# S5's two state scans issued at other places of the program, and HGRN2's scan steps taken in pairs

## The chip, the cores and the metric

The kernel runs on one core of one Trainium2 chip. The metric is device time in microseconds (us) of one execution, lower is better. A program of a core runs on five queues in parallel: PE (TensorE, matrix products), DVE (VectorE), ACT (ScalarE), POOL (GpSimd) and SP (SyncE, here only a queue that issues DMAs). POOL's queue carries DMA issues besides its arithmetic. Within a queue the instructions run in the order in which the program issued them; between queues they wait for one another by semaphores.

## What is computed

One inference step of a decoder of two layers, on 512 prompt positions and 64 sample positions (8 sequences of 8), 576 columns in all, width 1024, everything in float32. Layer 0 mixes tokens with HGRN2, layer 1 with S5. After the mixer, each layer has a SwiGLU and a per-layer embedding:

```python
def s5_mixer(x, h0_re, h0_im, ..., w_glu):
    bu = jnp.einsum('btgc,gpc->btgp', u, b_bar)            # 64 groups x 64 complex states
    bu = bu.at[:, 0].add(lam_bar * h0)
    _, h = lax.associative_scan(s5_combine, (a_el, bu), axis=1)   # h_t = lam_bar h_(t-1) + bu_t
    y = jnp.einsum('btgp,gcp->btgc', h, c_mat).real + d_skip * u
    y = jax.nn.gelu(y.reshape(bsz, t, D_MODEL))
    val, gate = jnp.split(y @ w_glu, 2, axis=-1)
    return val * jax.nn.sigmoid(gate), h_last.real, h_last.imag

# layer i, mixer = hgrn2 for i = 0, s5 for i = 1
x = layer_norm(ALPHA * x + mixer(x))
x = layer_norm(ALPHA * x + swiglu(x))
x = x + rms_norm((p_i @ w_proj) * sigmoid(x @ w_gate))
```

HGRN2 is a gated linear recurrence per head (8 heads of 128), computed chunkwise: products within a chunk, a state carried from chunk to chunk, and for the samples one step from the given states.

## The kernel before

**Matmuls and weights.** Every float32 weight product is made of three passes over a high and a low part (`mm3`, L295 to L299: L296 is high by high, L297 high weight by low activation, L298 low weight by high activation). A weight slot is 128x1024 numbers: a DMA loads it (`w_dma`, L217), ACT copies out the high part (`whi`, `w_conv`, L226), DVE subtracts to get the low part (`wlo`, `w_rest`, L250), and `w_rest` issues the DMA of a later slot at once. When these are issued is counted in products: `passed(n)`, called after each product, advances a counter, and conversions come due by it. The raw tile has two buffers, the converted slots a ring of `R_W` = 5 ("base") and, inside `more_weights`, some more ("ext", `WX` = 3 here). The first gated tiles of S5 use slots 118 to 125 of the weight order; slots 118 to 122 sit in the base ring, 123 to 125 in the ext ring, whose memory lies where the pools `op_pool` and `outer` lay.

**HGRN2 (from the start to about 340 us).** `hgrn()` projects head after head (`proj`), one yield for each `mm3`: 88 for an even head (it also makes V for two heads), 48 for an odd one. Meanwhile the scan of the head before is a generator (`scan`, L650), stepped after the yields whose numbers stand in `SCAN_AT` (first tuple for even h, second for odd). Its steps: 1 transposes four chunks of K2 (L658), copies them on ACT to `kT` and masks V on POOL; 2 transposes the samples' chunk (L665); 3 multiplies kT by V (L671) and carries the state; 4 and 5 make the sample states (L685); 6 to 9 make the attention of four chunks (L701, L706); 10 masks it on DVE (L710) and multiplies the sample queries (L716); 11 to 16 finish the head (L722 to L757). Head 7's scan runs later, after another list.

**S5 (about 890 to 1020 us).** The columns lie in two blocks of 288 (36 chunks of 8 positions). The stage runs in this order of the program, in `layer0_to_1`:

1. `z_part(0, o)` for eight octets of groups: products that give the chunks' inputs of block 0.
2. Block 0's scan, four quarters of 16 groups: `turn` (four DVE operations that rotate by a table), `run_on` (one DVE scan instruction and, where due, a copy of lengths), `turn` back.
3. Tiles `pj1` and `U`, loads of block 1's inputs, `ple_proj` (L964): 16 steps of two `mm3` and one ACT copy each, for the embedding of layer 1.
4. The DMA of the sample states `h0`, issued on POOL (L1620), then `z_part(1, o)`.
5. `last_samples`: h0 is scaled into the columns of block 0 (L1629), advanced on DVE, scaled on ACT and stored.
6. `lag_part(o)`, eight octets (L1471), copied out of PSUM by ACT; block 1's scan is the generator `last_states` (two yields for a quarter, nine steps in all), stepped after octets by `SL`.
7. `out_part(0, o)`, eight octets (L1444 with the states of block 0): DVE adds the product (`u<-u,mm`), ACT takes the GELU, SP writes it to DRAM and reads it back transposed, ACT and POOL split it into `xh` and `xl`. Block 1's scan is stepped after octets by `SO0`; what is left of it runs after the loop.
8. The gated tiles: for block and m, 48 passes (two units of 24) and `val * sigmoid(gate)`. Tiles (0,0) and (0,1) are multiplied at once in four PSUM banks (`GG` = 4). There are four banks in all for such products. At tile (0,3) `out_part(1, o)` comes first; it needs the states of block 1's scan.

The scan generator, whose steps are moved:

```python
        def last_states():
            for q in range(4):
                turn(1, q, True)
                run_on(1, q)
                yield
                turn(1, q, False)
                yield
            advance(po, chunk_state(63), ZL[:, :, 8])
            ...
            yield
```

Of the kernel before, what the change touches and what calls it, by code (L numbers as in the profile page):

```python
# [62 lines left out]
SY = ((6, 8), (8, 8), (6, 10), (6, 2))  # L63
QY = ((3, 3), (2, 5), (1, 3), (1, 2))
SPLIT_S5 = 14
SCAN_AT = ((2, 4, 10, 16, 20, 26, 30, 34, 38, 42, 46, 50, 54, 60, 68, 74), (2, 4, 6, 9, 12, 15, 17, 19, 21, 23, 26, 33, 34, 36, 41, 45))
QWAIT = 9
SIDE = 1
OCT = 1
TB = 3  # L70
SL = (0, 0, 1, 0, 1, 0, 1, 0)
SO0 = (0, 1, 0, 1, 0, 1, 0, 1)
YD = 4
WX = 3
AB = 2
GS = 3
SW = 64
GG = 4
LNEXP = "natural_log_exp_and_others"
# [60 lines left out]
def hybrid_decoder_kernel(ctx: ExitStack, tc: tile.TileContext, a: dict):  # L140
# [10 lines left out]
    def mm_bank():  # L151
        return bank("mm", 4)
# [110 lines left out]
    @contextmanager  # L263
    def more_weights(bufs, limit):

        with tc.tile_pool(name="wx", bufs=bufs) as pool:
            rings["ext"] = [pool, bufs, bufs, limit]
            yield
            assert pos["freed"] >= limit
            del rings["ext"]  # L270
# [3 lines left out]
    def take(n):  # L274
        p = pos["i"]
        pos["i"] += n
        return p
# [74 lines left out]
    def run(g):  # L352
        for _ in g:
            pass

    def step(g, n=1):
        for _ in range(n):
            if next(g, StopIteration) is StopIteration:
                return False
        return True  # L360

    def cols(blk):
        return slice(blk * NB, blk * NB + NB)
# [106 lines left out]
    def hgrn():  # L470
# [52 lines left out]
        def proj(h):  # L523
            if h % 2 == 0:
                p = take(16)
                V[h // 2] = hp.tile([128, 5, 256], FP32, tag="V", name="V", bufs=2)
                for i in range(5):
                    c = slice(i * 128, i * 128 + 128) if i < 4 else slice(T - 128, T)
                    ps = mm_bank()
                    for k in range(KD):  # L530
                        hi, lo = w_ap(p + 2 * k, 256)
                        mm3(ps[:, :256], xhih[:, k, c], xloh[:, k, c], hi, lo, k == 0, k == KD - 1)
                        yield
                    copy(V[h // 2][:, i, :], ps[:, :256])
                free_to(p + 16)
            d = hd[h] = {}

            yield from two_units(take(8))
            sides.append(decay(h, d, hd["ps"]))

            yield from two_units(take(8))
            sides.append(factors(d, hd["ps"]))
            yield from two_units(take(8))
            sides.append(queries(h, d, hd["ps"]))
# [217 lines left out]
        for h in range(H):  # L762
            at = SCAN_AT[h % 2]
            for n, _ in enumerate(proj(h)):
# [199 lines left out]
    def ple_proj(pj, pin):  # L964
        hi, lo = pin
        p = take(16)
        for m in range(KD):
            for blk in range(2):
                ps = mm_bank()
                run(unit(ps[:, :NB], p + 2 * m, [0, 1], lambda k, b: hi[:, k, cols(b)],  # L970
                         lambda k, b: lo[:, k, cols(b)], blk))
                copy(pj[:, m, cols(blk)], ps[:, :NB])
                yield
            free_to(p + 2 * m + 2)
# [540 lines left out]
    def turn(blk, q, back):  # L1515

        gs, n = slice(16 * q, 16 * q + 16), slice(1, 36 if blk else KA + 1)
        h, c, C, Z = (x[:, n] if len(x.shape) == 2 else x[:, :, n] for x in
                      (HS[blk][:, gs], s5["c"], s5["C"][:, gs], s5["Z"][:, gs]))
        tt(c[0:64], h[64:128], Z[64:128], OP.mult)  # L1520
        tt(c[64:128], h[0:64], Z[0:64], OP.mult)
        tt(h, h, C, OP.mult)
        tt(h, h, c, OP.add if back else OP.subtract)
# [5 lines left out]
    def run_on(blk, q):  # L1529
        h = HS[blk][:, 16 * q:16 * q + 16].rearrange("p g k -> p (g k)")  # L1530
        nc.vector.tensor_tensor_scan(h, s5["rho"][q % 2].rearrange("p g k -> p (g k)"), h, 0.0,
                                     op0=OP.mult, op1=OP.add)
        if (blk, q) < (1, 2):
            lengths((q + 2) % 4)
# [3 lines left out]
    def layer0_to_1():  # L1538
        right, wide, outer = ExitStack(), ExitStack(), ExitStack()
# [28 lines left out]
        op_pool = ExitStack()  # L1568
# [24 lines left out]
            elif o > 1:  # L1593
                step(tails[1], 2)
        settle(1)
        for q in range(4):
            turn(0, q, True)
            run_on(0, q)
            turn(0, q, False)
        left.close()  # L1600
        pj1 = left.enter_context(tc.tile_pool(name="pp1", bufs=1)).tile([128, KD, T], FP32, name="pj1")
        work = ExitStack()
# [10 lines left out]
        def samples(tag, n=1):  # L1613
            t = s5["zp"].tile([128, n, NG, 8], FP32, tag=tag, name="sm")
            return [t[:, i] for i in range(n)]

        proj = ple_proj(pj1, s5["pin"])
        run(proj)
        h0, = samples("phi")
        nc.gpsimd.dma_start(h0, a["h0"])  # L1620
# [34 lines left out]
        scan = last_states()  # L1655
# [10 lines left out]
        for o in range(8):  # L1666
            lag_part(o, mg[o])
            if o >= OCT:
                cl.append(octet(s5["zq"], cl_d, len(cl), "zw", 8))
            step(scan, SL[o])  # L1670
        for o in range(8):
            out_part(0, o, cl[o])
            y_start(0, o)
            step(scan, SO0[o])
            if o >= YD:
                step(y_loads[0, o - YD])
        y_start(0, 8)
        y_start(0, 9)
        for o in range(8 - YD, 8):
            step(y_loads[0, o])  # L1680
        run(scan)

        ln = None
        op_pool.close()
        outer.close()
        gp = work.enter_context(tc.tile_pool(name="gp", bufs=1))
        p0, pss = take(128), []
        with more_weights(WX, (p0 + 128) // 8):
            for blk, m in [(b, m) for h in (0, 4) for b in range(2) for m in range(h, h + 4)]:
                p = p0 + 16 * m  # L1690
                if (blk, m) == (0, 3):
                    st.update(queue=nc.sync, load=LOAD_MM, split=SPLIT_MM)
                    for n in range(8):
                        out_part(1, n, cl[n])
                        y_start(1, n)
                    y_start(1, 8)
                    y_start(1, 9)
                    wide.close()
                    ln = open_norm(3, 4, False)
                    for n in range(m):  # L1700
                        ln[0].added(n)
                while len(pss) < 2:
                    new = [mm_bank() for _ in range(1 if blk or m else GG)]
                    go(units([ps[:, :NB] for ps in new], p + 8 * len(pss), list(range(KD)), x_hi, x_lo, blk))
                    pss += new
                psv, psg = pss[:2]
                pss = pss[2:]
                if blk == 1:
                    free_to(p + 16)
                if (blk, m) == (0, 3):  # L1710
                    for n in range(KD):
                        step(y_loads[1, n])
                s = gp.tile([128, NB], FP32, tag="gs", name="gs", bufs=GS)
                tables()
                act(s, psg[:, :NB], ACT.Sigmoid)
                tt(s, s, psv[:, :NB], OP.mult)
                residual(m, blk, s)
                if ln:
                    ln[blk].added(m)
# [176 lines left out]
```

## Time and profile before

| | us |
|---|---|
| median of 3 runs | 1583.01 (1582.04 to 1585.63) |
| the profiled execution, its own time | 1582.62 |
| its span, first to last instruction | 1580.8 |
| PE busy in it | 1512.7 (96%) |
| DVE busy | 947.3 (60%) |
| ACT busy | 687.4 (43%) |
| POOL busy | 314.9 (20%) |
| mean granted clock of TensorE | 0.985 |

The profile comes from one execution. Its times count from the first instruction. Busy time is that in which an engine ran an instruction; PE's matmuls overlap in the records, so what PE is worth is better read from the distance between starts. The granted clock is given as a share of 2.4 GHz: 1.00 is that, 0.50 is 1.2 GHz, and a value between them is a mean over a stretch with both. An arrow behind an idle time names what ended it.

### The profile page before, as it was taken

What the parts mean: (1) busy time and instruction counts of PE and PEld (TensorE: products, weight loads), DVE (VectorE), ACT (ScalarE), POOL (GpSimd) and SP (SyncE); (2) the same over time, 40 slices, a digit from 0 to 9 for tenths busy, and PEclk for the clock granted to TensorE, in tenths of its full rate; (3) what the DMA queues carried; (4) which work ended last, traced back from release to release, by engine and by line L of the source; (5) the groups of instructions that cost most, each with busy time, mean ns of one, the idle gap of its engine ahead of it and who ended that gap; (6) DMA issues with size and microseconds to landing.
All of it is one profiled execution on the core that took longest, in us unless ns stands there. A gap on an engine that the chain in (4) does not pass through costs nothing.

```text
span 1580.8 us, 30046 instructions
## 1 busy us (share of the span) xinstructions
PE 1512.7 (96%) x12550; PEld 1464.3 (93%) x12550; DVE 947.3 (60%) x1725; ACT 687.4 (43%) x1151; POOL 314.9 (20%) x433
## 2 busy tenths in 40 slices
PE   7999999899999999999999857999999999999998
PEld 7898989788999999999999857999999999999997
DVE  4848484868547778963486789557433233334685
ACT  5646464746532223222268533537431232123375
POOL 1303030202103758860022202102000000000111
PEclk9999999999999999999999988999999999999999
DMA  5213132232224887663314985432222222223121
GB/s 186 96 69 109 56 109 69 96 115 80 68 70 139 218 189 216 194 180 109 107 54 148 234 251 162 108 101 81 68 84 94 77 80 94 81 81 120 32 76 60
DMA packets 97367, 180.32 MB, mean 114 GB/s; under 512 B 42016, under 2 KB 57040, under 8 KB 96976
## 3 DMA queue, kind: packets, MB, share of 16 engines
q1 hardware_dynamic: 88288, 151.95, 31.7%
q0 software_dynamic: 8944, 26.46, 6.0%
q8 instruction: 98, 1.61, 0.4%
q14 instruction: 37, 0.30, 0.1%
HBM read 151.08 MB, written 27.30 MB: 113 GB/s over the span
## 4 chain that ended last, share of the span: by engine, by line
PE 77%; DVE 12%; ACT 5%; issue 3%; DMA 1%; POOL 1%; SPq 0%; DVEq 0%; POOLq 0%; ACTq 0%
PE mm L296 24%; PE mm L297 24%; PE mm L298 23%; DVE b L577 1%; DVE wlo L200 1%; DVE xf L200 1%; ACT whi L197 1%; PE tr L706 1%; DVE xl L200 1%; DVE K L200 1%; DVE ln_q L200 1%; DVE ln_z L200 1%; DVE cross L200 1%; PE mm L1444 1%; PE tr L671 1%
## 5 line engine op out<-in xcount | busy, mean ns | idle before, releaser
L296 PE MATMUL mm<-xh,whi 128*128 128x288 f32 x2048 | 609.3, 297 | 8.5 <-ACT xh L197 6.6
L297 PE MATMUL mm<-xl,whi 128*128 128x288 f32 x2048 | 608.1, 297 | 4.3 <-POOL xl L200 2.8
L298 PE MATMUL mm<-xh,wlo 128*128 128x288 f32 x2048 | 606.1, 296 | 1.3 <-DVE wlo L200 1.3
L296 PEld LDWEIGHTS mm<-xh,whi 128*128 128x128 f32 x2048 | 387.7, 189 | 14.8 <-ACT xh L197 7.8
L297 PEld LDWEIGHTS mm<-xl,whi 128*128 128x128 f32 x2048 | 387.4, 189 | 7.6 <-POOL xl L200 4.4
L298 PEld LDWEIGHTS mm<-xh,wlo 128*128 128x128 f32 x2048 | 387.3, 189 | 1.5 <-DVE wlo L200 1.5
L197 ACT ACTIVATE whi<-wraw 128x1024 fp32r<-128x1024 f32 x208 | 218.6, 1053 | 257.7 <-DMA wraw<-in_w_dram 124.9
L200 DVE TENSOR_TENSOR wlo<-wraw,whi 128x1024 fp32r<-128x1024 f32 x208 | 256.3, 1249 | 33.9 <-ACT whi L197 33.5
L296 PE MATMUL mm<-hhi,whi 128*128 128x288 f32 x704 | 209.3, 297 | 0.0
L298 PE MATMUL mm<-hhi,wlo 128*128 128x288 f32 x704 | 207.5, 295 | 0.0
L297 PE MATMUL mm<-hlo,whi 128*128 128x288 f32 x704 | 207.3, 294 | 0.0
L200 DVE TENSOR_TENSOR fs<-fs,mm 128x288 f32<-128x288 f32 x88 | 39.9, 453 | 253.7 <-PE mm L298 241.1
L200 POOL TENSOR_TENSOR ln_s<-ln_s,xf 128x288 f32<-128x288 f32 x24 | 24.2, 1010 | 570.1 <-DVE xf L200 451.0
L296 PEld LDWEIGHTS mm<-hhi,whi 128*128 128x128 f32 x704 | 132.1, 188 | 1.7 <-issue 1.4
L297 PEld LDWEIGHTS mm<-hlo,whi 128*128 128x128 f32 x704 | 132.1, 188 | 0.3
L298 PEld LDWEIGHTS mm<-hhi,wlo 128*128 128x128 f32 x704 | 132.0, 188 | 0.0
L296 PE MATMUL mm<-xhi,whi 128*128 128x320 f32 (+1 forms) x384 | 120.8, 315 | 0.0
L297 PE MATMUL mm<-xlo,whi 128*128 128x320 f32 (+1 forms) x384 | 112.8, 294 | 0.0
L298 PE MATMUL mm<-xhi,wlo 128*128 128x320 f32 (+1 forms) x384 | 112.7, 294 | 0.0
L197 ACT ACTIVATE hhi<-fs 128x288 fp32r<-128x288 f32 x88 | 38.9, 442 | 151.1 <-DVE fs L200 151.1
L194 ACT ACTIVATE fs<-mm,eps 128x288 f32<-128x288 f32 x88 | 44.1, 501 | 130.2 <-PE mm L298 129.9
L296 PEld LDWEIGHTS mm<-xhi,whi 128*128 128x128 f32 x384 | 72.1, 188 | 6.8 <-issue 4.4
(316 smaller groups left out, 2235.4 us busy)
## 6 DMA issues: line engine op xcount, KB each, us to landing
wraw<-in_w_dram SPq DMA_DIRECT2D x198, 512.0 KB
wraw<-in_w_dram POOLq DMA_DIRECT2D x10, 512.0 KB, 5.0
S<-in_s_dram SPq DMA_DIRECT2D x8, 512.0 KB
out_hgs_dram<-So SPq DMA_DIRECT2D x8, 512.0 KB
wr<-wt_scratch SPq DMA_DIRECT2D x16, 256.0 KB
bT<-in_s5bt_dram SPq DMA_DIRECT2D x16, 256.0 KB
cl_scratch<-cl POOLq DMA_DIRECT2D x16, 256.0 KB, 5.3
zw_scratch<-zw POOLq DMA_DIRECT2D x16, 256.0 KB, 6.2
```

Of the source, the lines that this page charges most:

```text
L194: nc.scalar.activation(out, in_, func, bias=ZERO if bias is None else bias, scale=scale)
L197: nc.scalar.activation(out, in_, ACT.Copy)
L200: (eng or nc.vector).tensor_tensor(out, x, y, op=op)
L296: nc.tensor.matmul(out, whi, rhi, start=start, stop=False)
L297: nc.tensor.matmul(out, whi, rlo, start=False, stop=False)
L298: nc.tensor.matmul(out, wlo, rhi, start=False, stop=stop)
L577: nc.vector.tensor_tensor_scan(b[l], segm[l], L, 0.0, op0=OP.mult, op1=OP.add)
L671: nc.tensor.matmul(ps[:, j * 128:j * 128 + 128], kT[:, j, :], Vh[:, j, :], start=True, stop=True)
L706: nc.tensor.matmul(ps[s0:s0 + l, o + s0 + l:o + s0 + 2 * l], KL[:, q0:q0 + l], QL[:, q0:q0 + l], start=True, stop=True)
L1444: nc.tensor.matmul(ps[r:r + 64, c], w[:, j, r:r + 64], xo[:, c], start=True, stop=True)
```

## The change

Two independent edits. In HGRN2, eight entries of `SCAN_AT` change, so that steps 1 and 2, 6 and 7, 8 and 9, 12 and 13 are taken together at one yield. In S5, the first block's scan is issued after the tiles and loads of point 3 and its pieces alternate with two steps of `ple_proj` each; of the second block's nine scan steps one stays in the lag products (`SL`), four are issued after the products of gated tile (0,0) (`SG`), ahead of that tile's gating, and the rest before the gating of tile (0,1). The pools `op_pool` and `outer` are closed, and the ext ring opened, only after that; one gating buffer less (`GS`) makes the room.

```diff
-SCAN_AT = ((2, 4, 10, 16, 20, 26, 30, 34, 38, 42, 46, 50, 54, 60, 68, 74), (2, 4, 6, 9, 12, 15, 17, 19, 21, 23, 26, 33, 34, 36, 41, 45))
+SCAN_AT = ((4, 4, 10, 16, 20, 26, 26, 34, 34, 42, 46, 54, 54, 60, 68, 74), (4, 4, 6, 9, 12, 15, 15, 19, 19, 23, 26, 34, 34, 36, 41, 45))
...
-SL = (0, 0, 1, 0, 1, 0, 1, 0)
-SO0 = (0, 1, 0, 1, 0, 1, 0, 1)
+SL = (0, 0, 1, 0, 0, 0, 0, 0)
+SG = 4
...
-GS = 3
+GS = 2
...
-        for q in range(4):
-            turn(0, q, True)
-            run_on(0, q)
-            turn(0, q, False)
         left.close()
...
         proj = ple_proj(pj1, s5["pin"])
+        for q in range(4):
+            turn(0, q, True)
+            run_on(0, q)
+            step(proj, 2)
+            turn(0, q, False)
+            step(proj, 2)
         run(proj)
...
         for o in range(8):
             out_part(0, o, cl[o])
             y_start(0, o)
-            step(scan, SO0[o])
...
-        run(scan)
 
         ln = None
-        op_pool.close()
-        outer.close()
         gp = work.enter_context(tc.tile_pool(name="gp", bufs=1))
         p0, pss = take(128), []
-        with more_weights(WX, (p0 + 128) // 8):
+        with ExitStack() as more:
...
                 psv, psg = pss[:2]
                 pss = pss[2:]
+                if (blk, m) == (0, 0):
+                    step(scan, SG)
+                if (blk, m) == (0, 1):
+                    run(scan)
+                    op_pool.close()
+                    outer.close()
+                    more.enter_context(more_weights(WX, (p0 + 128) // 8))
```

## Rows read from the trace of the kernel before

**Rows 1.** The page's first part: busy us, share of the span, instructions.
```profile
PE 1512.7 (96%) x12550; PEld 1464.3 (93%) x12550; DVE 947.3 (60%) x1725; ACT 687.4 (43%) x1151; POOL 314.9 (20%) x433
```

**Rows 2.** Stretches: length, busy (count) of PE, PEld, DVE, ACT, POOL, clock, DMA, GB/s.
```profile
935.00:940.00 5.00, 0.00 (x0) 0.00 (x0) 4.07 (x6) 0.00 (x0) 1.61 (x3) 0.58 0.51 179
...
950.00:955.00 5.00, 5.00 (x122) 5.00 (x120) 4.83 (x7) 2.77 (x7) 0.53 (x1) 0.71 0.72 239
...
975.00:980.00 5.00, 4.70 (x19) 4.70 (x20) 4.85 (x7) 2.07 (x5) 2.69 (x3) 0.50 0.67 133
980.00:985.00 5.00, 5.00 (x38) 5.00 (x38) 4.92 (x4) 1.34 (x3) 3.84 (x4) 0.98 0.31 50
```

**Rows 3.** Waits of PE over the whole span: us in total, times, longest us.
```profile
PE mm L1471 <- ACT zl L197: 12.8, 1, 12.8
PE tr L658 <- DVE K L200: 7.9, 4, 2.5
```

**Rows 4.** DVE's timeline, 907 to 948 us: start us, us, what, [idle before <-releaser].
```profile
907.80 1.74 DVE L200 TENSOR_TENSOR cross<-xl,xh 64x448 f32<-64x448 f32 x2
...
936.65 2.35 DVE L200 TENSOR_TENSOR wlo<-wraw,whi 128x1024 fp32r<-128x1024 f32 x2
...
942.85 0.48 DVE L1629 TENSOR_SCALAR xl<-sm,sgn 128x512 f32<-128x512 f32 x1 [3.72 <-DMA sm<-in_h_dram]
...
946.92 1.22 DVE L200 TENSOR_TENSOR wlo<-wraw,whi 128x1024 fp32r<-128x1024 f32 x1
```

**Rows 5.** POOL's timeline, 908 to 939 us.
```profile
938.16 0.53 POOL L223 DMA_DIRECT2D wraw<-in_w_dram  x1 [29.23 <-DVE wlo L200]
```

**Rows 6.** ACT's timeline, 929 to 988 us.
```profile
942.13 1.06 ACT L197 ACTIVATE whi<-wraw 128x1024 fp32r<-128x1024 f32 x1 [13.29 <-DMA wraw<-in_w_dram]
...
947.03 0.81 ACT L194 ACTIVATE sm<-sm,eps,sgn 128x512 f32<-128x512 f32 x1 [3.48 <-DVE sm L200]
...
986.10 2.01 ACT L197 ACTIVATE whi<-wraw 128x1024 fp32r<-128x1024 f32 x2 [3.59 <-DVE xl L200]
```

**Rows 7.** DVE's timeline, 948 to 990 us: block 1's scan and what lies between.
```profile
948.16 1.49 DVE L200 TENSOR_TENSOR cross<-xl,xh 64x560 f32<-64x560 f32 x2
...
953.09 1.49 DVE L200 TENSOR_TENSOR cross<-xl,xh 64x560 f32<-64x560 f32 x2
...
961.00 0.81 DVE L200 TENSOR_TENSOR u<-u,mm 128x288 f32<-128x288 f32 x2
...
975.64 2.00 DVE L200 TENSOR_TENSOR cross<-xl,xh 64x560 f32<-64x560 f32 x2
...
984.06 1.23 DVE L200 TENSOR_TENSOR xl<-xl,turn 128x560 f32<-128x560 f32 x1
...
987.55 0.26 DVE L1651 TENSOR_SCALAR po<-po,sgn 128x64 f32<-128x64 f32 x1
```

**Rows 8.** PE's timeline, 930 to 1004 us: lag products, output products of block 1.
```profile
948.20 8.44 PE L1471 MATMUL mm<-u,zw 128*64 128x72 f32 x192 [3.36 <-ACT u L197]
...
996.52 7.66 PE L1444 MATMUL mm<-xl,zw 128*64 128x64 f32 x256
```

**Rows 9.** PE's timeline in an odd head of HGRN2, 126 to 138 us.
```profile
126.86 0.66 PE L658 MATMUL tr<-cst,K 128*128 128x128 f32 x4 [1.79 <-DVE K L200]
...
129.22 1.05 PE L671 MATMUL tr<-V,kT 128*128 128x128 f32 x8
...
136.86 0.38 PE L701 MATMUL tr<-QH,KH 128*128 128x128 f32 x2
...
137.66 0.42 PE L296 MATMUL mm<-xhi,whi 128*128 128x320 f32 x1
137.92 0.31 PE L297 MATMUL mm<-xlo,whi 128*128 128x320 f32 x1
```

**Rows 10.** ACT's timeline at the same place, 126 to 131 us.
```profile
127.48 1.05 ACT L197 ACTIVATE whi<-wraw 128x1024 fp32r<-128x1024 f32 x1
128.43 0.87 ACT L197 ACTIVATE kT<-tr 128x512 f32<-128x512 f32 x2
```

## The prediction

> **What bounds the kernel now.** Read first the busy times [rows 1]: PE works nearly the whole span, so a change of 0.2% has to come from PE's idle or slow stretches, or go into them. Second, a table of the busy times by 20 us: outside HGRN2 and S5 PE is full almost everywhere, and between 900 and 980 us it is not, while DVE is. Third, PE's waits: the longest one stands at the lag products of S5, 12.8 us, and the transposes of K in HGRN2 wait 7.9 us in four odd heads [rows 3]. Fourth, the timelines of the other engines at these two places, to see what is late.
>
> In S5, DVE is late. It starts block 0's scan at 907.80 and has it done at 936.65; two weight subtractions were issued behind it [rows 4]. POOL's next weight load waits 29.23 us for the first of them [rows 5], and the load of h0 stands behind that one on POOL. So DVE then waits 3.72 us for h0 [rows 4], and ACT waits 13.29 us for the late weight slot, with the copies of the last input products behind it, which PE needs: that is the 12.8 us [rows 6, 3]. After that ACT scales the samples at 947.03 [rows 6], PE resumes the lag products at 948.20 [rows 8], and DVE does block 1's scan from 948.16 to 987.81 with eight output additions in between [rows 7]. The next two weight slots (123, 124) wait for the scan's last use of the turn tables, 986.10 [rows 6], and the output products of block 1 start at 996.52 [rows 8]. From there PE only waits for what these products set off, so this start is what I follow: **whatever moves 996.52 moves the end.**
>
> **The change part by part, S5.**
> *First block's scan.* It has the same operations, and the projections that it alternates with need nothing of it (their weight slots are subtracted before 907.80), so the scan itself wins nothing. What moves is the order on DVE: one of the two subtractions (2.35 us for both [rows 4]) falls before the scan's last quarter (three of four of 28.85), about 930 instead of 937. POOL's load and h0 behind it start some 7 us earlier. DVE's total up to the samples is unchanged, 28.85 + 2.35, so it gets there at 939.1 as before, but finds h0 there: minus 3.7 us. Bounds: 0 if h0's load, sharing the DMA engines with the lag weights, lands as late as now; minus 3.7 is all of the wait. I take minus 3.7, since 7 us of lead stand against a load that took 4 (issued behind 938.16 [rows 5], there at 942.85 [rows 4]). ACT then scales at 943.4, PE resumes the lag products at 944.5 and needs their 8.44 us [rows 8]: done at 953.0. Bounds of that term: 8.44 has half its time at 1.2 GHz, as the clock 0.71 of that stretch shows [rows 2]; at full clock the 192 would take some 2.5 us less. PE is idle before it now too, so I keep 8.44.
>
> *Second block's scan.* DVE does the subtraction at 943.4 (1.22 [rows 4]), then the one step left in the lag products (948.16 to 953.09, 4.93 [rows 7]), and is done at 949.5. Behind it in DVE's queue stand the eight output additions, which wait for PE: products from 953.0, 7.66 us for 256 [rows 8], last addition 0.9 us later, 961.6. So DVE sits through 12.1 us with 3.6 us of work (two additions take 0.81 [rows 7], plus the gaps): **8.5 us of idle DVE that the kernel before filled with scan steps.** Then come the other eight steps: 39.65 (948.16 to 987.81) less 3.5 for the additions less 4.93, which is 31.2, with tile (0,0)'s two gating operations between them, 0.9. End of scan: 961.6 + 32.1 = 993.7, against 987.81, plus 5.9.
>
> *From the end of the scan to the output products of block 1.* Before: 996.52 - 987.81 = 8.7 us, because both units of tile (0,2) (48 passes of 0.132 us, 38 in 5 us [rows 2]) had to come after it. After: the first unit needs slot 122, which is converted early, and runs under the scan. The second needs slot 123, whose memory is free only when the scan has read its tables (1.7 us ahead of its end [rows 6, 7]). ACT copies its high part by 993.1, DVE finishes the scan, gates tile (0,1) (0.9) and subtracts (1.2): 995.8. Then 22 passes, 2.9 us. That is 5.0 us after the scan instead of 8.7. But PE has been idle for some 6 us by then, and here such a gap ends at 1.2 GHz: in 935 to 940 PE is empty and the clock 0.58, and 975 to 980 takes 19 passes where 980 to 985 takes 38 [rows 2]. Some 14 of the 22 at half clock add 1.9: 6.9 us. Bounds: 5.0 (no drop) to 8.8 (the slow clock lasts into the output products).
>
> Sum for S5: +5.9 + 6.9 - 8.7 = **+4.1 us**. With the lower bounds 5.9 - 2.5 + 5.0 - 8.7 = -0.3; with h0 late +4.1 + 3.7 = +7.8.
>
> Covers and queues. The tiles' loads on SP that now come before the scan need nothing from it. On SP the store of the final states moves from 987.8 to 993.7; behind it stand the stores of block 1's outputs, due only after 1000. On ACT the copies of slots 123 and 124 wait for the scan, and behind them stands tile (0,2)'s sigmoid only. POOL's splits of the eight inputs still fall beside the scan. One gating buffer less costs nothing while a tile takes PE 6.3 us and its gating on ACT and DVE about 1.5.
>
> **HGRN2.** No operation is added. *Steps 1 and 2:* in odd heads the transposes move back by two products, some 0.8 us of PE work (six passes of 0.132 [rows 2]). The wait of 1.79 for K [rows 9] shrinks by that. But kT's copy on ACT stands behind a weight copy and starts at 128.43 [rows 10], and the product with kT starts at 129.22 [rows 9]; now PE would be there at 128.4 and wait for the copy until about 129.07. Gain 0.15 in four heads: 0.6. Bounds: 0 to 3.2 (0.8 in four heads, if the copy were earlier). *The other pairs:* a group of attention products takes 0.80 (136.86 to 137.66), and the first pass behind it 0.26 to the next start [rows 9] instead of 0.132 [rows 2]. If pairing saves this whole excess, it is 0.13 in 3 pairs of 7 heads, 2.7 us; if the second group pays the same on its own entry, nothing. I take 0.05 each, 1.0, nearer to nothing since the second group's short products hide no weight load either. A loss of as much as 1 us isn't excluded: PE reaches a waiting group sooner. HGRN2: **-1.6 us**, from -5.9 to +1.
>
> **Rivals.**
> *A. Faster: HGRN2's waits go.* If kT's copy is done before PE arrives (it decides at 128.4 against the weight copy's end at 128.5 [rows 10]) and the pairs save the whole excess, HGRN2 gives -5.9, and S5 without the clock loss +2.2: -3.7, 1579.3. For it: the wait is real and deterministic. Against it: ACT's queue.
> *B. S5 comes out even.* If the lag products run at full clock: -0.3 - 1.6 = -1.9, 1581.1. Against it: PE's idle time ahead of them remains.
> *C. Slower: h0 lands late.* If the two loads that POOL now issues earlier share the DMA engines with the lag weights to the point that h0 is no earlier than 942.85, DVE waits as before and nothing pays for its new idle time: +2.5 + 3.7 = +6.2, 1589.2. It decides at 939.2. For it: the DMA share of 935 to 940 is still 0.51 [rows 2]. Against it: 7 us of lead.
> *D. Slower: DVE and POOL collide more.* Six of DVE's scan operations from 975.64 to 984.06 are 0.49 us longer than their like, 2.9 us, beside 6.5 us of POOL [rows 7, 2]. If DVE paid all of POOL's time, the scan would end 3.6 later: +6.1, 1589.1. The Trainium skill ("SBUF — State Buffer", Who interferes with whom) states such a rule: of two such operations the second to issue blocks fully. The trace shows less than half of it.
>
> **How the numbers follow.** Forecast: 1582.62 (the profiled execution) + 4.1 - 1.6 = 1585.1; it stands 0.4 below the median of the runs, so 1585.5. Its own range is 1583 to 1588. A measurement of this kernel tells about 0.2%, 3.2 us, from no change. Chances: forecast 0.42, A 0.20, B 0.15, C 0.18, D 0.05. Faster by over 0.2%: A and a little of B, 0.22. Slower: C, D, and 0.16 of the forecast, 0.39. Same: the rest, 0.39. The range leaves out the outer half of A and some of C and D: 1579 to 1589.
>
> **What would show it.** Right: POOL's wait of 29 us is some 22; DVE no longer waits for h0; a DVE gap of several us stands before the output additions; block 1's scan ends near 994 and its output products start near 1000; PE has two idle stretches before that, with the clock at 0.50; L658's wait in odd heads halves while L671 gets a wait for kT. Wrong: the products start at or before 996, or the first 340 us shrink by over 3 us.

## The result, and the profile after

| | before | after |
|---|---|---|
| median of 5 runs, us | 1583.66 (1582.04 to 1588.70) | 1593.71 (1593.04 to 1595.66) |
| ratio, 95% interval | | 1.0062 (1.0046 to 1.0078) |
| the profiled execution, us | 1582.62 | 1595.66 |
| its span, us | 1580.8 | 1593.9 |

The changed kernel is 0.62% slower, some 10 us. Its profiled execution is the longest of the five, so what follows accounts for 13.1 us of span, 3 of them more than the medians show. The forecast was 1585.5, its range 1579 to 1589.

The busy time on the page of the changed kernel (busy us, share, instructions) has the work of [rows 1] almost unchanged; PE's is 4.4 us more:

```profile
PE 1517.1 (95%) x12550; PEld 1467.7 (92%) x12550; DVE 947.5 (59%) x1725; ACT 688.2 (43%) x1151; POOL 314.1 (20%) x431
```

PE's waits in the changed kernel (us in total, times, longest), against [rows 3]:

```profile
PE mm L296 <- ACT whi L197: 13.0, 1, 13.0
PE mm L1471 <- ACT zl L197: 8.8, 1, 8.8
...
PE tr L658 <- DVE K L200: 5.6, 4, 2.8
PE mm L1444 <- issue: 4.3, 3, 3.2
...
PE tr L671 <- ACT kT L197: 2.7, 5, 0.8
```

The wait at the lag products fell by 4.0 and HGRN2's wait for K by 2.3, with the wait for kT in its place. Two are new: 13.0 for a weight's high part, and 3.2 in the output products (L1444) that the view calls "issue".

What DVE did, answering [rows 4, 7] (start us, us, what, idle before and what ended it):

```profile
905.43 1.74 DVE L200 TENSOR_TENSOR cross<-xl,xh 64x448 f32<-64x448 f32 x2
...
937.78 0.48 DVE L1632 TENSOR_SCALAR xl<-sm,sgn 128x512 f32<-128x512 f32 x1 [1.09 <-DMA sm<-in_h_dram]
...
952.20 0.46 DVE L200 TENSOR_TENSOR u<-u,mm 128x288 f32<-128x288 f32 x1 [4.18 <-PE mm L1444]
...
961.21 0.46 DVE L200 TENSOR_TENSOR u<-u,mm 128x288 f32<-128x288 f32 x1 [4.19 <-PE mm L1444]
...
964.36 0.45 DVE L200 TENSOR_TENSOR u<-u,mm 128x288 f32<-128x288 f32 x1 [0.99 <-PE mm L1444]
964.85 1.99 DVE L200 TENSOR_TENSOR cross<-xl,xh 64x560 f32<-64x560 f32 x2
...
997.22 0.26 DVE L1654 TENSOR_SCALAR po<-po,sgn 128x64 f32<-128x64 f32 x1
```

The first block's scan starts 2.4 us earlier; h0 costs 1.1 instead of 3.7; then DVE idles between output additions (13.2 us in all between 948.0 and 964.8), does the rest of the second block's scan from 964.85, and starts its last operation at 997.22 instead of 987.55.

POOL's weight load, answering [rows 5], and its first splits beside block 1's scan:

```profile
928.65 0.53 POOL L223 DMA_DIRECT2D wraw<-in_w_dram  x1 [22.08 <-DVE wlo L200]
...
965.41 3.36 POOL L200 TENSOR_TENSOR xl<-u,xh 128x288 fp32r<-128x288 f32 x3 [19.13 <-ACT xh L197]
```

ACT's late weight copy, the samples, and the copies of slots 123 and 124, answering [rows 6]:

```profile
936.40 1.06 ACT L197 ACTIVATE whi<-wraw 128x1024 fp32r<-128x1024 f32 x1 [9.27 <-DMA wraw<-in_w_dram]
941.97 0.81 ACT L194 ACTIVATE sm<-sm,eps,sgn 128x512 f32<-128x512 f32 x1 [4.15 <-DVE sm L200]
...
995.79 2.00 ACT L197 ACTIVATE whi<-wraw 128x1024 fp32r<-128x1024 f32 x2 [14.55 <-DVE xl L200]
```

PE, answering [rows 8]: lag products, output products of block 0 in three pieces, the second unit of tile (0,2), output products of block 1:

```profile
943.13 7.94 PE L1471 MATMUL mm<-u,zw 128*64 128x72 f32 x192 [4.03 <-ACT u L197]
950.91 1.79 PE L1444 MATMUL mm<-xl,zw 128*64 128x64 f32 x54
953.19 3.89 PE L1444 MATMUL mm<-xl,zw 128*64 128x64 f32 x126 [0.48 <-issue]
960.31 3.96 PE L1444 MATMUL mm<-xl,zw 128*64 128x64 f32 x76 [3.23 <-issue]
...
996.90 0.61 PE L296 MATMUL mm<-xh,whi 128*128 128x288 f32 x1 [12.96 <-ACT whi L197]
999.52 0.61 PE L298 MATMUL mm<-xh,wlo 128*128 128x288 f32 x1 [1.77 <-DVE wlo L200]
...
1004.99 7.66 PE L1444 MATMUL mm<-xl,zw 128*64 128x64 f32 x256
```

And the clock beside it, by 5 us (columns as [rows 2]):

```profile
985.00:990.00 5.00, 0.00 (x0) 0.00 (x0) 4.82 (x8) 0.00 (x0) 0.00 (x0) 0.77 0.00 2
990.00:995.00 5.00, 0.00 (x0) 0.00 (x0) 4.83 (x6) 0.00 (x0) 0.00 (x0) 0.50 0.00 0
995.00:1000.00 5.00, 1.33 (x4) 0.98 (x5) 4.24 (x10) 2.00 (x2) 0.22 (x1) 0.50 0.03 7
1000.00:1005.00 5.00, 5.00 (x24) 4.83 (x23) 0.00 (x0) 0.00 (x0) 0.34 (x1) 0.52 0.29 105
```

PE stands empty behind DVE, the clock goes to 1.2 GHz (0.50), and tile (0,2) runs the 24 passes of its second unit almost all at that level.

The span splits at three points: the start of block 0's scan (all that happens before it), the first output product of block 1, and the end of ACT's last split of block 1's outputs (`xh`, read back from DRAM). The starts of that scan lie between 905.3 and 909.5 us in kernels whose program is the same up to there, so distances from it say more than times, and what a single profile has ahead of it says little. All in us, one profiled execution each; the labels are those of the next sections (left out are the three kernels in which PE does not wait for slot 123, whose products start in another way):

| kernel | scan start | to block 1's products | to the last split | to the end | last two together |
|---|---|---|---|---|---|
| before | 907.80 | 88.72 | 17.67 | 566.61 | 584.28 |
| after | 905.43 | 99.56 | 21.02 | 567.89 | 588.91 |
| e1_pairs | 909.44 | 88.45 | 18.35 | 566.66 | 585.01 |
| e2_first | 908.38 | 86.06 | 17.83 | 566.63 | 584.46 |
| e4_pairs_first | 907.86 | 85.39 | 17.50 | 566.65 | 584.15 |
| e13_best_hold | 905.57 | 85.37 | 19.19 | 567.57 | 586.76 |
| e3_second | 910.34 | 99.55 | 19.60 | 568.61 | 588.21 |
| e5_pool | 906.77 | 98.24 | 20.67 | 567.72 | 588.39 |
| e6_cl | 908.14 | 92.37 | 20.72 | 569.67 | 590.39 |
| e7_fill | 908.04 | 92.00 | 20.03 | 568.23 | 588.26 |
| e9_mix | 909.12 | 88.48 | 22.09 | 567.81 | 589.90 |
| e10_hold | 905.90 | 97.64 | 20.76 | 569.60 | 590.36 |
| e15_early_conv | 909.53 | 97.91 | 20.14 | 569.72 | 589.86 |
| e14_early | 909.04 | 97.69 | 18.21 | 566.66 | 584.87 |
| e16_early_cl | 905.95 | 92.25 | 19.03 | 567.97 | 587.00 |
| e17_hold_pool | 905.44 | 95.94 | 18.56 | 566.86 | 585.42 |

So after against before: -2.4 up to the scan, +10.8 to block 1's products, +4.6 behind them: +13.1, with rounding.

The changed kernel's row is at the slow end of what its program does. e5_pool, e10_hold and e17_hold_pool have the same program up to block 1's products, and there they take 98.24, 97.64 and 95.94 where it takes 99.56. The kernels derived from it below are 1 to 6 us faster against it in this table (the two parts behind the scan's start together) than in their medians, some 3 us on average. So the +10.8 is one reading of something between 7 and 11 against this profile of before, and gains are better read from the medians.

### The profile page after: what moved, and what is told of

Read it like the earlier page. It is cut to its first block, busy times and chain, and to the rows that moved or that the text cites. A ratio compares the mean times of both kernels' runs of the same rounds, so it can differ in the third digit from the quotient of the medians.

```text
span 1593.9 us, 30044 instructions
## 1 busy us (share of the span) xinstructions
PE 1517.1 (95%) x12550; PEld 1467.7 (92%) x12550; DVE 947.5 (59%) x1725; ACT 688.2 (43%) x1151; POOL 314.1 (20%) x431
## 4 chain that ended last, share of the span: by engine, by line
PE 75%; DVE 12%; ACT 6%; issue 3%; DMA 3%; POOL 1%; SPq 0%; DVEq 0%; ACTq 0%; POOLq 0%
PE mm L296 23%; PE mm L297 23%; PE mm L298 23%; DVE b L577 1%; DVE wlo L200 1%; ACT whi L197 1%; DVE xf L200 1%; DMA wraw<-in_w_dram 1%; DVE xl L200 1%; PE tr L706 1%; DVE cross L200 1%; DVE ln_q L200 1%; DVE ln_z L200 1%; PE mm L1444 1%; PE tr L671 1%
## 5 line engine op out<-in xcount | busy, mean ns | idle before, releaser
L296 PEld LDWEIGHTS mm<-xh,whi 128*128 128x128 f32 x2048 | 388.6, 190 | 23.7 <-ACT whi L197 13.2
```

Of the source, the lines that this page charges most:

```text
L296: nc.tensor.matmul(out, whi, rhi, start=start, stop=False)
```

## Experiments: the parts alone

Differences between kernels below are those of their ratios times 1584; each ratio carries about 0.15%, so two kernels have to stand some 3 us apart, unless they ran on the same chip and their runs don't overlap.

**The scan steps of HGRN2 alone.** Edit: only the two lines of `SCAN_AT`.

> The kernel before with the new SCAN_AT alone (the step pairs of HGRN2). Theory: the profile of the changed kernel starts S5's first scan 2.4 us earlier (905.43 instead of 907.80), so the pairs gain about 2.4 us and nothing later takes it back: ratio 0.9985. Rival: the gain is lost in the later layers or the pairs are neutral: ratio 1.000. A second rival, that the pairs cost part of the 10 us: over 1.001.

Measured: 1582.41, ratio 0.9986 (0.9976 to 0.9996): 2.2 us faster. In the trace the wait for K falls from 7.9 to 5.9 and that for kT rises from 0.8 to 2.4, much as in the changed kernel. Its profiled execution (1584.69) is one of its slower ones and shows nothing of the gain, its scan in S5 starting at 909.44.

**Block 0's scan between the projections alone.** Edit: the same lines as in the change, block 1's scan as before.

> The kernel before with block 0's scan between the projection steps alone. Theory: one weight subtraction and h0's load come 7 us earlier, the samples' scaling on ACT is some 2.7 us earlier after the start of the scan (36.5 instead of 39.2 us in the profile of the changed kernel), and since the vector engine then has block 1's scan to do without a gap, the output products of block 1 start 2 to 2.7 us earlier: ratio 0.9985. Rival: the interleaving is the harmful part (the pieces wait for the projections or delay them): 2 us or more slower, ratio over 1.001.

Measured: 1580.70, ratio 0.9975 (0.9963 to 0.9988): 4.0 us faster. DVE's wait for h0 is 1.13 instead of 3.72; block 1's products come 2.7 us earlier behind the scan's start.

**Block 1's scan alone.** Edit: `SL`, `SG`, `GS`, the steps beside the tiles and the later opening of the ext ring, all else as before.

> The kernel before with block 1's scan moved beside the gated tiles alone (SL, SG, GS and the later closing of the pools). Theory: this part costs all of the loss and more: idle DVE during the output products of block 0, and the rest of the scan on the path of tile (0,2): 12 to 15 us slower than before, ratio 1.008 to 1.010. Rival, the first block's part is the harmful one: within 3 us of before.

Measured: 1597.22, ratio 1.0079 (1.0062 to 1.0096): 12.5 us slower. So this part alone is what makes the change slow. One piece of it, the gating buffer given up (`GS`), has no run of its own. In the changed kernel's trace ACT's sigmoids of tiles (0,0) to (0,2) (at 979.94, 980.74 and 1005.10) all wait for PE's products and none for such a buffer.

**Without block 1's scan.** Edit: the two other parts together.

> The kernel before with the step pairs and block 0's scan between the projections, block 1's scan as before. Theory: the two gains add, 4 to 5 us faster than before, ratio 0.997, and it is the fastest of the four. Rival, block 0's part harmful: no faster than before.

Measured: 1578.76, ratio 0.9964 (0.9951 to 0.9978): 5.7 us faster than before, and faster than the changed kernel by 15. It beats both. The parts don't quite add: 12.5 less 5.7 is 6.8, and the change costs 9.8, a gap at the edge of what can be told. A later kernel (e13_best_hold, below) turned out to be this program a second time: 1579.44, ratio 0.997 (0.9956 to 0.9984).

## Experiments: what block 1's scan costs

**The constants of block 0's output products.** Each octet's products need a constant tile of 512 KB. SP issues these loads as the lag products free the buffers (eight issues from 927.58 to 951.4). Here one tile serves all octets, and seven of the eight loads are left out.

```diff
-                cl.append(octet(s5["zq"], cl_d, len(cl), "zw", 8))
+                cl.append(cl[0])
```

> The changed kernel, with one of the eight loads of output coefficients used for all octets; seven loads of 512 KB are left out, so the output products use wrong coefficients. Theory: block 0's output products, no longer held back by these loads, take 7.7 to 8.5 us instead of 13.4, the scan's remaining steps start 5 us earlier and so does all behind them: 4.5 to 5.5 us faster than the changed kernel, ratio to before 1.003. Rival: the products wait for their banks or for instruction fetch: 13 us as now, ratio 1.006.

Measured: 1590.35, ratio 1.0035 (1.0023 to 1.0048): 4.3 us faster than the changed kernel, just under the 4.5 to 5.5 expected. PE's timeline has block 0's products in one piece:

```profile
952.78 7.61 PE L1444 MATMUL mm<-xl,zw 128*64 128x64 f32 x256
```

That is the 7.66 of [rows 8], against 13.4 (950.91 to 964.27) above: the pauses called "issue" are waits for these loads. (13.4 is the most that any profile has: in the six other kernels with the same program up to there, e5_pool, e10_hold, e11_slot, e14_early, e15_early_conv and e17_hold_pool, these products take 10.1 to 11.3.) In the table block 1's products come 7.2 us sooner; the rest behind them is 1.5 longer, which is within what one profile tells.

**DVE kept at work there.** Edit: one more scan step in the lag products, one in the output products, two instead of four at tile (0,0).

```diff
-SL = (0, 0, 1, 0, 0, 0, 0, 0)
-SG = 4
+SL = (0, 0, 1, 0, 1, 0, 0, 0)
+SO0 = (0, 0, 0, 0, 1, 0, 0, 0)
+SG = 2
...
+            step(scan, SO0[o])
```

> The changed kernel with two of the second scan's steps put back: one more in the lag products, one after the fourth octet of block 0's output products; two instead of four after tile (0,0)'s products, the rest where it is. Theory: the two steps (3.06 and 4.93 us) fall into DVE's two idle gaps of 4.2 us, so block 1's scan ends 7 to 8 us earlier and the kernel is 6 to 8 us faster than the changed one: ratio to before 1.001 to 1.002. Rival, what costs is that tile (0,2) has to wait for the scan at all, or the weight loads on SP: 2 us or less, ratio 1.005.

Measured: 1591.23, ratio 1.0038 (1.0025 to 1.005): 3.8 us faster than the changed kernel, less than the 6 to 8 expected. PE still pauses for the constants, but DVE has a step to do in the pause (958.00 to 962.9):

```profile
952.60 5.42 PE L1445 MATMUL mm<-xl,zw 128*64 128x64 f32 x180
961.20 3.69 PE L1445 MATMUL mm<-xl,zw 128*64 128x64 f32 x76 [3.19 <-issue]
```

Block 1's products come 7.6 us sooner behind the scan's start. That fits the reading that the loads cost time because DVE had been left without work beside them, but it doesn't prove it: the other step fills the gap ahead of the products (4.18 us in the changed kernel), which e6_cl has too, and no run fills the pause alone.

**The second unit of tile (0,2).** It needs slot 123, whose memory is free when the scan is done. Here PE multiplies by slot 122 again.

```diff
-go(units(..., p + 8 * len(pss), ...))
+go(units(..., p + 8 * len(pss) * ((blk, m) != (0, 2)), ...))
```

> The changed kernel whole, but the second unit of gated tile (0,2) multiplies by slot 122 again instead of slot 123 (so the gate half of that tile is another product; the conversions of slot 123 stay as they are, only PE does not wait for them there). Theory: the wait for the slot whose memory the scan frees is what stands between the scan's end and block 1's output products; without it these start right behind the scan's last operation on the states, about 994.5 instead of 1005.0, partly at half clock, and the run is 6 to 8 us faster than the changed kernel, 1586 to 1588, ratio 1.001 to 1.002. Rival (PE would wait there anyway, for slot 124 or the gating): under 3 us faster, 1591 or more, ratio 1.0045 or more.

Measured: 1589.32, ratio 1.0038 (1.0026 to 1.005): 3.8 us faster, on the same chip as e10_hold (1593.08 to 1595.74 against 1587.89 to 1592.23, no overlap); less than the theory's 6 to 8, more than the rival's. Of block 1's products PE does the first octet (32) at 989.42; its row of the next six:

```profile
998.79 7.63 PE L1444 MATMUL mm<-xl,zw 128*64 128x64 f32 x192 [8.23 <-DVE gs L200]
```

They start 89.4 behind the scan's start, where in the changed kernel the first start at 99.6, but now wait for a PSUM bank that DVE frees with tile (0,1)'s gating, behind the scan; and the first of them run at half clock: 192 take 7.63 here, where 256 take 7.66 otherwise. So the waits form a row: slot 123, then the bank, both behind the same scan.

**DVE filled and the end of the scan split.** Edit: the scan steps spread as before over the lag products, one in the output products, two at tile (0,0), two at (0,1), the final states after (0,2), weight loads on POOL until tile (1,0).

> The changed kernel with DVE kept busy: scan steps after octets 2, 4 and 6 of the lag products and after octet 3 of block 0's output products, two after tile (0,0)'s products, two before tile (0,1)'s gating, the last (the final states) after tile (0,2)'s; weight loads on POOL until tile (1,0). Theory: DVE has no idle stretch, the scan ends as early as in the kernel with pairs and the first block's part alone, and only one of tile (0,2)'s two units comes after it: 6 to 8 us faster than before, ratio 0.9955. Rival: the second block's steps beside the gated tiles cost in any place: slower than 0.9964, the ratio of the kernel with pairs and the first block's part.

Measured: 1587.88, ratio 1.0023 (1.0014 to 1.0032): 6.2 faster than the changed kernel, and still slower than before, where 6 to 8 faster than before was expected: the rival came. Block 1's products now start as early as before (88.48), and yet the time is 3.6 us longer. That leaves the last column of the table: 589.9 instead of 584.3.

## Experiments: what comes behind block 1's products

In the changed kernel ACT converts slot 125 between the GELUs of block 1, and SP issues the loads of slots 126 and 127, 512 KB each, between the stores and reads of block 1's outputs (at 1008.11 and 1010.53). Before, POOL had issued them by 995.56, ahead of the stores.

**Another queue.** Edit: these loads stay on POOL until tile (1,0).

> The changed kernel, with the two weight loads that now come due during block 1's output products (slots 126 and 127) issued on POOL's queue instead of SP's: the switch of the queue comes at tile (1,0). Theory: on SP they stand between the stores and the reads of block 1's outputs, each waits for a subtraction, and that makes the stretch from the end of these products to the last split 14.2 us instead of 10.9: 3 to 4 us faster than the changed kernel, so 6 to 7 us slower than before (ratio 1.004). Rival: it is the two loads' bandwidth and not their place in the queue: no faster than the changed kernel (1.006).

Measured: 1595.19, ratio 1.0064 (1.005 to 1.0077): nothing won. The loads move at the same time, from another queue.

**Held back.** Edit: loads that fall due from tile (0,3) on are counted, and issued at tile (1,0).

> The changed kernel whole, with one thing moved: the DMAs of weight slots 126 and 127 (512 KB each), which it issues between the stores and reads of block 1's outputs, are issued only with gated tile (1,0); nobody needs these slots before tile (0,4). Theory: they cost time as bytes, not as entries of a queue; with them gone the stretch from the end of block 1's output products to the last split falls from 14.2 us back to about 10.9, and the run is 3 to 3.5 us faster than the changed kernel, about 1590.4, ratio near 1.004. Rival (the read-back is slow for another reason, the late and half-speed start): no change, 1593.7, ratio 1.006.

Measured: 1594.16, ratio 1.0067 (1.0055 to 1.0079): nothing won. But the edit didn't do what it was for. SP waits for no tile; it came to the held loads right behind the last reads, which were still under way:

```profile
1017.79 2.36 SPq L1489 DMA_DIRECT2D u<-y_scratch  x3
1020.32 0.98 SPq L226 DMA_DIRECT2D wraw<-in_w_dram  x2
```

The last split starts 4.1 us behind the last read's issue (1019.8 to 1023.9), where it is 2.7 in the changed kernel.

**Early.** Edit: ahead of tile (0,2)'s gating the due conversions are issued, and with them the loads, on POOL.

```diff
+                if (blk, m) == (0, 2):
+                    while rests:
+                        w_rest()
+                    w_conv(True)
+                    w_rest()
```

> The changed kernel whole, with the low part of slot 124 and both parts of slot 125 issued ahead of tile (0,2)'s gating instead of between the output products of block 1, so that the loads of slots 126 and 127 are issued there too (on POOL, where the kernel before has them). Theory (conversions and loads among the GELUs, stores and reads of block 1 cost the 4.4 us that the stretch from the first output product of block 1 to the end is longer): 588.9 falls to 584.5 to 585.5 us, and the time to 1589.3 to 1590.3, ratio 1.0035 to 1.004. Rival (the stretch is slow for what PE did before it, its late start and clock): 1593 to 1594, ratio 1.006.

**Early conversions, late loads.** As before it, with the two loads issued on SP behind the stores of octets 0 and 2.

> As e14_early, but the loads of slots 126 and 127 stay where the changed kernel has them, on SP behind the first and third store of block 1's outputs. If the conversions on ACT and DVE are what delays the stores, 1589.3 to 1590.5 as e14_early; if it is the loads, 1593 to 1594 as the changed kernel; if both share it, between.

Measured, on the same chip: 1591.54 (1588.20 to 1593.39), ratio 1.0041, and 1595.80 (1593.80 to 1599.06), ratio 1.007: the runs don't overlap, so it is the loads and not the conversions. The early version won 3.3 us, a little less than expected in time, and its stretch of the table is where it was expected. POOL's issues of the early version:

```profile
1002.72 0.53 POOL L223 DMA_DIRECT2D wraw<-in_w_dram  x1 [0.55 <-DVE wlo L200]
1007.68 0.53 POOL L223 DMA_DIRECT2D wraw<-in_w_dram  x1 [4.44 <-DVE wlo L200]
```

The stretch from 1008 to 1030 us of the same kernel, the clock third from the end:

```profile
1008.00:1030.00 22.00, 20.61 (x319) 19.72 (x316) 7.90 (x18) 10.16 (x19) 3.42 (x5) 1.00 0.59 133
```

And that stretch where only the conversions are early:

```profile
1008.00:1030.00 22.00, 19.98 (x322) 18.19 (x317) 8.09 (x19) 10.86 (x20) 3.18 (x4) 0.94 0.66 157
```

With the loads ahead, the last two columns of the table are those of before (584.87). With them in the read-back it takes 2 us longer to the last split, PE waits for splits, the clock falls, and 3 more are lost behind it.

**Held behind the splits.** As e10_hold, but the held loads go to POOL, whose queue reaches them behind its last split.

> As e10_hold, but the two held loads are issued on POOL, whose queue reaches them only behind its last split of block 1's outputs, so no byte of them moves beside the stores and reads. If bytes beside the read-back are the cost, the stretch from the first output product of block 1 to the end falls from 588.9 us to 585 to 586.5 (the conversions stay among the GELUs), and the time to 1590.0 to 1591.5 as in e14_early. Rival (the early conversions were what helped in e14_early, the loads only when far ahead): no change from the changed kernel and e10_hold, 1593.7 to 1594.2.

Measured: 1591.02 (1588.61 to 1595.65), ratio 1.0046 (1.0032 to 1.0061): 2.5 us faster than the changed kernel, in time and in the table inside what was expected of bytes as the cause. In time this is at the edge of what can be told; the trace, of the fastest of its nine runs, has it (585.42 in the table, clock 1.00 from 1008 to 1030):

```profile
1020.02 0.79 POOL L200 TENSOR_TENSOR xl<-u,xh 128x288 fp32r<-128x288 f32 x1 [1.31 <-ACT xh L197]
1020.76 1.09 POOL L226 DMA_DIRECT2D wraw<-in_w_dram  x2
```

**The best kernel with held loads.** e4_pairs_first with the same holding.

> Paired steps and block 0's scan between the projections, block 1's scan where the kernel before has it, and in addition the loads that fall due beside block 1's outputs issued only with tile (1,0). Theory: here the loads land before the stores and reads of block 1's outputs, so that holding them wins at most 0.5 us: 1578.3 to 1578.8, ratio 0.9960 to 0.9965. Rival (these loads slow the read-back in every version): 2 to 3 us faster, 1576, ratio 0.9945.

Measured: 1579.44. In that kernel all three loads fall due ahead of block 1's products, so nothing was held and its program is that of e4_pairs_first. As a repetition it shows how far one profile can be trusted: 586.76 against 584.15 in the last column. Kernels with loads in the read-back lie at 588.2 and above, those without at 587.0 and below.

**Do the costs add up?** First early loads and the one constant tile together:

> e14_early with one constant tile for all eight output products of each block (seven loads of 512 KB left out, so the outputs are other numbers). The two costs lie in different stretches, so they should add: 1593.7 less 4.4 (e6_cl) and 3.5 to 4.4: 1585 to 1586, ratio 1.001 to 1.0015. Rival (what one gives is lost again in the next wait): no faster than e6_cl, 1590, ratio 1.0035.

Measured: 1591.03, ratio 1.004 (1.0025 to 1.0056), no faster than e6_cl or e14_early alone, as the rival had it. Its runs spread from 1586.95 to 1592.63, and the profiled one is the lowest, so its row in the table (92.25, 587.0) shows both gains while the median shows one. Why these runs spread more stays open, and with it whether the two gains add.

Then the three together (one constant tile, slot 122 in tile (0,2), the loads held), at first with the holding that had failed:

> The changed kernel with three of its costs taken away together: one constant tile serves all eight output products of each block (seven loads of 512 KB left out, so the outputs are other numbers), the second unit of tile (0,2) multiplies by slot 122, and slots 126 and 127 are loaded with tile (1,0). Theory (these three are all that moving the second scan costs): 1593.7 less 4.4, 6 to 8 and 3 to 3.5, so 1577 to 1580, ratio 0.996 to 0.998, the time of the kernel that leaves the second scan where it was and has the other parts of the change (1578.8). Rival (something else is in it): 1584 or more, ratio 1.000 or more.

Measured: 1586.68, ratio 1.0015 (1.0004 to 1.0026): the rival came. And with the loads behind POOL's last split:

> As e12_all (one constant tile for all output products, the second unit of tile (0,2) on slot 122, so the outputs are other numbers), with the held loads behind POOL's last split. If the three causes are all that the move of the second scan costs, 1579 to 1582.5, near the kernel that leaves that scan in place (1578.8), ratio 0.9965 to 0.999. Rival (more is in it): as e12_all, 1585 to 1587, ratio 1.0005 to 1.0015.

Measured: 1583.39, ratio 0.9997 (0.9984 to 1.0009): 10.3 us faster than the changed kernel, of the 15.5 that lie between it and e4_pairs_first; it falls between the theory and its rival. The three causes are two thirds of the cost. What remains is, by this run's trace, the scan's end itself: DVE sits idle 5.1 us ahead of block 0's first addition, ends the scan at 992.9, 86.5 behind its start where before it was 80.0, and block 1's products wait 9.7 us for the bank that tile (0,1)'s gating behind it frees. No run tests this rest.

## Why the prediction was wrong, step by step

**HGRN2, -1.6: within its range.** e1_pairs measured -2.2 (-0.6 to -3.8). The wait for kT appeared as forecast, and the two waits together fell by 0.4 (K -2.0, kT +1.6) for the forecast 0.6. What the other pairs gave, put at 1.0, no run separates.

**Block 0's scan: right.** POOL's wait is 22.08 for the forecast 22, DVE's wait for h0 is 1.09 where none was forecast, and e2_first measured -4.0 (-1.9 to -5.9) for the forecast -3.7.

**Block 0's output products: the step that failed first.** The prediction took 7.66 for them, a row of block 1 [rows 8], whose constants have long been loaded. Block 0's arrive while it multiplies; 13.4 us, last addition 59.4 behind the scan's start where 53.8 was forecast (961.6 - 907.80), and DVE idle for 13.2 us instead of 8.5. With the loads out (e6_cl) it is 52.8: the sum was right but for this row. The trace of before had it. There the same products, in PE's timeline, come in four pieces and take 10.9 us, 956.47 to 967.36:

```profile
956.47 1.79 PE L1444 MATMUL mm<-xl,zw 128*64 128x64 f32 x54
959.03 4.21 PE L1444 MATMUL mm<-xl,zw 128*64 128x64 f32 x126 [0.76 <-issue]
963.69 0.55 PE L1444 MATMUL mm<-xl,zw 128*64 128x64 f32 x12 [0.45 <-issue]
965.30 2.06 PE L1444 MATMUL mm<-xl,zw 128*64 128x64 f32 x64 [1.07 <-DVE u L200]
```

Two of the pauses are "issue", as above; the prediction read past them. DVE had scan steps to do beside them, with no idle time in its timeline from 948.16 to 987.81, and these are the steps that the change moves away. So of the S5 term that came out 6.7 us too small (+10.8 measured, +4.1 forecast), 5.6 are this one in the profile. With the 10.1 to 11.3 us of the six kernels alike the row was 2.4 to 3.6 too small, and taking the loads away won 4.3 us in the median: the step failed in each, by some 2 to 6 us.

**The rest of the scan and the slot behind it: right.** 32.6 us for the forecast 32.1. The collisions with POOL came as priced: the two operations at 964.85, beside POOL's splits, take 1.99 where their like take 1.49 [rows 7]. Rival D, by which DVE pays all of POOL's time, did not come. The Trainium skill ("SBUF — State Buffer", Who interferes with whom) calls the port pair that DVE and POOL share an exclusive lock; the trace again shows less than that, 0.50 us for the pair of operations, while POOL's splits (from 965.41) lie beside it for 1.4 us. From the end of the scan to block 1's products 7.5 for the forecast 6.9, with nearly all passes at half clock instead of 14 of 22.

**Behind block 1's products: missed.** The prediction said that from there PE only waits for what these products set off, and followed the start alone. It counted the conversions of slots 123 and 124, which the scan holds up, but not the loads that they set off and where these would now run, so that this stretch stood in the sum at nothing: 4.6 us. e14_early against e15_early_conv shows that the loads are the cause (4.3 us in the medians); one profile of this stretch is good to some 2.6 us, as e13_best_hold shows, so the 4.6 are known no better than that.

Together 6.7 + 4.6 - 0.8 (HGRN2) are the 10.5 us by which the profiled execution (1595.66) missed its sum (1585.1). By the medians the miss is 8.2 (1593.71 against 1585.5): by the experiments 4.3 of it are block 0's constants and 2.5 to 4.3 the loads in the read-back, if the two add, which e16_early_cl doesn't bear out.

**The rivals.** None of the four came. C had DVE wait for h0, which came early. The case that did come, that loads set DVE's idle time and not products, was not among them.

## What to carry to other kernels

Before a filler is moved away from a place, find out what it filled: where a stretch of products is longer than its like elsewhere in the same trace, look for a wait in it (or a lower clock), even where the view has no better word for it than "issue". When a conversion or a buffer's release moves, follow the DMAs that it triggers to the place where they now run, and look whether that place is bound by DMA. And take the duration of a step from its own row, not from its like at another place.

## What the runs showed of the chip

While block 1's outputs are stored and read back, the DMA engines are nearly all busy at a modest rate. In e4_pairs_first (DMA share, then GB/s, at the end of the row):

```profile
1004.00:1008.00 4.00, 4.00 (x33) 4.00 (x32) 0.79 (x2) 1.34 (x3) 0.81 (x1) 1.00 0.92 181
```

That is more of the DMA engines for less than in 950 to 955 of the kernel before, 239 GB/s at a share of 0.72 [rows 2]. 1 MB of weights beside it cost some 2 to 3 us until the last split (18.21 in e14_early, 20.14 in e15_early_conv, 21.02 in the changed kernel), from POOL's queue (e5_pool, 20.67) as from SP's. And small waits were followed by a second cost: in the changed kernel PE waits only 0.3 to 0.5 us at a time for splits at 1020 to 1026, yet the clock falls:

```profile
1020.00:1024.00 4.00, 2.99 (x11) 1.70 (x11) 0.92 (x2) 1.19 (x4) 0.79 (x1) 1.00 0.89 178
1024.00:1028.00 4.00, 3.14 (x11) 2.59 (x12) 0.78 (x2) 2.85 (x5) 1.59 (x2) 0.66 0.24 37
```

The granted clock of the 6 us behind the last split goes with the table's column "to the end". It is 1.00 in before, e1, e2, e4, e14 and e17 (566.6 to 566.9 to the end), 0.70 to 0.78 in after, e3, e5, e7, e9, e13 and e16 (567.6 to 568.6), and 0.50 to 0.52 in e6, e10 and e15 (569.6 to 569.7). Every kernel of the table with loads in the read-back has such a dip, but e13_best_hold (0.74) and e16_early_cl (0.72) have it without them: e13_best_hold is e4_pairs_first a second time, so what brings the dip about is not settled by the loads alone.
